# Second gate of a hybrid decoder layer: eight columns in the first feed-forward part instead of ten, their four sums at other output pairs, six columns beside the output projection

## The chip, the cores and the metric

One core of one Trainium2 chip runs the kernel. The metric is the device time of one execution in microseconds (us); the time of a kernel is the median of its runs. The profile shows one execution, instruction by instruction, with the engines TensorE (PE), VectorE (DVE), ScalarE (ACT), GpSimd (POOL) and SyncE (SP, which issues most of the DMAs).

## The reference, cut to what matters

```python
mod_all = jnp.einsum('bd,ldm->lbm', jax.nn.silu(c), w_ada) + b_ada[:, None, :]
sh1, sc1, g1, sh2, sc2, g2 = jnp.split(mod_all[l], 6, axis=-1)
h = modulate(rms_norm(x, norm1_g[l]), sh1, sc1)
u = h @ w_in[l]                      # convolution group and attention group
...
x = x + g1[:, None, :] * (mixed @ w_out[l])
h = modulate(rms_norm(x, norm2_g[l]), sh2, sc2)
x = x + g2[:, None, :] * (jnp.square(jax.nn.relu(h @ w_ff1[l])) @ w_ff2[l])
return rms_norm(x, normf_g)
```

There are 512 tokens of 2048 features in float32, and the feed-forward width is 8192. The second gate g2 has 2048 numbers. In the kernel they are 16 columns of 128 (one number per partition), kept in the last 16 columns of the tile `mod`. Each column is 128 dot products of a row of `w_ada` with SiLU(c), and the weights of one column are 1 MB. Nothing needs g2 before the end of the second feed-forward product, where it scales what is added to x.

## The kernel before, in words

The layer runs in three stages, each with an `Order` of its own: projections with convolution and values; attention; and then output projection with both feed-forward parts. Every operation is first recorded by `Order.record` (so that nearly all instructions have one line, L144, in the profile, and are told apart by their tiles), and `Order.emit` then calls a planner, `Order.plan`, that fixes the order of instructions on each engine. Tensor operations keep the order in which they were recorded. The others are taken when they are ready by the planner's own prices, and among those that are ready the one whose result is due first. For a DMA the planner counts its size at a fixed rate, a fixed latency, and `order.margin` on top: what reads the data is planned that much later. The third stage is planned in one pass. On the chip each engine then takes its instructions in the planned order and waits wherever something is not there yet.

Matmuls are done in three products of high and low halves (fp32r): ScalarE makes the high half of a weight block (`hl`), VectorE the low half. The feed-forward products use a Strassen-like scheme: seven block products for a 2 by 2 block product. The first feed-forward part makes 32 output pairs, p = 0 to 31: pairs 0 and 1 piece by piece ahead of the loop (`part`, `results_of`), pairs 2 to 31 in a loop over `ff1(p)`. One `ff1` loads four weight blocks of 512 KB through SP, adds two more to them in DMAs through POOL (up to p = 28; later pairs add on VectorE), runs 7 x 24 matmuls of 128x128 by 128x256, and stores its results to DRAM, through POOL.

The 16 columns of g2 are spread over the kernel:

- the first two (16 less `NLATE`) in the first stage;
- the columns from 16 less `NLATE` up to 16 less `NGATE` (the list `behind`) in `late_ada`, which is recorded first in the third stage and so runs beside the output projection. Each column takes two loads of 512 KB into four slots `wa`, and two VectorE dot products of 128x1024 (`dot`). The slots `wa`, and the two that hold SiLU(c), are used again later for the tokens of the feed-forward part (`tk`).
- the last `NGATE` in the loop over the pairs. `gate_part(s)` loads 256 KB of `w_gate` into the first half of the one tile `spare` (named `snap` in the trace) and adds its two halves, each times a column of SiLU(c), to one of the two running sums `gsums` in the second half of that tile. Eight parts make the sums of two columns, and `gate_sum(n)` lets TensorE add them over the partitions with a column of ones, after which VectorE adds the bias. The list `when` says behind which pair a part is recorded, and `sums` ahead of which pair a `gate_sum` is recorded, and so where it stands in TensorE's order.

`late_ada` and `gate_part` set `order.margin = MARGIN` around their loads.

With `NGATE` = 10 there are 40 parts and five sums, at p = 10, 15, 19, 24 and 28; `behind` has four columns.

Of the kernel before, what the change touches and what calls it, by code (L numbers as in the profile page):

```python
# [32 lines left out]
NWA = 8  # L33
NBANK = 6
NLATE = 14
NGATE = 10
NWARM = 3
SLACK = 4.0
MARGIN = 8.0
FAST = 378e3  # L40

V_BADA, V_N1, V_CW, V_CB, V_GC, V_GA, V_N2, V_NF, V_C, V_ID, V_END = \
# [272 lines left out]
def hybrid_layer(ctx: ExitStack, tc: tile.TileContext, a, out):  # L315
# [34 lines left out]
    def accum(name=None):  # L350
        return next(accums)
# [183 lines left out]
    for i in range(4):  # L535
# [8 lines left out]
        + [M_G2 * NK + k for k in range(NK - NLATE)]  # L544
    behind = [M_G2 * NK + k for k in range(NK - NLATE, NK - NGATE)]
    rb = accum("rb")
# [176 lines left out]
    def late_ada(n, slots):  # L723
# [4 lines left out]
        for k in range(n):  # L728
            m, acc = behind.pop(0), next(accs)
            for i in range(2):  # L730
                w = wa[(2 * k + i) % slots]
                order.margin = MARGIN
                nc.sync.dma_start(out=w, in_=a["w_ada"][2 * m + i])
# [123 lines left out]
    for j in range(8):  # L857
# [4 lines left out]
        for i in range(3):  # L862
            n = 3 * j + i
# [338 lines left out]
    def bankf():  # L1202
        return next(banks)
# [56 lines left out]
    for k in range(8):  # L1260
        wh, wl = oa[k] if k < 2 else hilo(hl_tile(16), raw_blob(a["w_oa"][k]))
        for i in range(8):
            s = slice(i * P, (i + 1) * P)
# [146 lines left out]
    def ff1(p):  # L1410
        raw = [raw_blob(a["w_f1"][p, b]) for b in range(4)]
        ps = {}
        x, y = temp((P, 2, HT), name="gx"), temp((P, 2, HT), name="gy")
        for i, w in enumerate(operands(raw, True, p % 4 == 3, add=[a["w_f1"][p, b] for b in (0, 3)] if p < 29 else None)):
            ch, first, last = CHAIN[i]
            if first:
                ps[ch] = bankf()
            run(ps[ch], w, tok[i], first, True)
            b = ps[ch][:, :HT]
            if i == B1:  # L1420
                p1 = next(p1s)
                nc.scalar.activation(p1, b, AF.Copy)
            elif i == U6:
                sub(y[:, 1], p1, b)
            elif i == T5:
                sub(y[:, 0], b, p1, OP.add)
            elif i == B2:
                nc.scalar.activation(x[:, 0], b, AF.Relu)
            elif i == T7:
                sub(y[:, 0], b, y[:, 0])  # L1430
            elif i == B3:
                sub(y[:, 1], b, y[:, 1], OP.add)
                nc.scalar.activation(y, y, AF.Relu)
                nc.scalar.activation(y, y, AF.Square)
            elif i == T4:
                sub(x[:, 1], b, p1)
                nc.scalar.activation(x[:, 1], x[:, 1], AF.Relu)
        nc.scalar.activation(x, x, AF.Square)
        outcome(p, x, y, [temp((P, 2, HT), name="gz") for _ in range(2)])
# [4 lines left out]
    NP = 2  # L1444
# [25 lines left out]
    def results_of(p):  # L1470
        x, y, z, v = [temp((P, 2, HT)) for _ in range(4)]
        for u in range(2):
            nc.scalar.activation(x[:, u], results[p, u][:, LO], AF.Relu)
            sub(y[:, 1 - u], firsts[p, u], results[p, u][:, HI], OP.add)
        nc.scalar.activation(x, x, AF.Square)
        nc.scalar.activation(y, y, AF.Relu)
        nc.scalar.activation(y, y, AF.Square)
        outcome(p, x, y, (z, v))

    def gate_part(s):  # L1480

        gsum, b = gsums[s // 8 % 2], s % 8
        order.margin = MARGIN
        nc.sync.dma_start(out=spare[:, :T], in_=a["w_gate"][s])
        order.margin = 0.0
        for j in range(2):
            w, c = spare[:, j * HT:(j + 1) * HT], sc[:, 2 * b + j:2 * b + j + 1]
            if b + j == 0:
                nc.vector.tensor_scalar(gsum, w, c, None, op0=OP.mult)
            else:  # L1490
                nc.vector.scalar_tensor_tensor(out=gsum, in0=w, scalar=c, in1=gsum, op0=OP.mult, op1=OP.add)

    def gate_sum(n):
        total, gsum = bankf(), gsums[n % 2]
        m = M_G2 * NK + NK - NGATE + 2 * n
        for i in range(2):
# [26 lines left out]
    for n in range(8, 16):  # L1523
        part(n)
        if n in (13, 15):
            results_of({13: 1, 15: 0}[n])
    when = [NP + 1 + s * 22 // (4 * NGATE) for s in range(4 * NGATE)]
    sums = [when[8 * n + 7] + 4 for n in range(NGATE // 2)]
    for p in range(NP, 32):
        if p in sums:  # L1530
            gate_sum(sums.index(p))
        ff1(p)
        for s in [s for s in range(4 * NGATE) if when[s] == p]:
            gate_part(s)
# [165 lines left out]
def _in_turn(np, m):  # L1700

    return np.arange(2 * m).reshape(2, m).T.reshape(-1)
# [21 lines left out]
def _layouts(np, x, c, w_ada, b_ada, norm1_g, w_in, conv_w, conv_b, cmp_pe_k, cmp_pe_v, cmp_w1_k,  # L1724
# [18 lines left out]
    d["xr"] = xt.reshape(NK // 2, P, 2, 2, T // 2)[..., _in_turn(np, W_F)].reshape(xt.shape)  # L1743
    early = D * 6 - P * NGATE
    d["w_ada"] = w_ada[0][:, :early].T.reshape(-1, P, 2, 1024).transpose(0, 2, 1, 3).reshape(-1, P, 1024)
# [51 lines left out]
```

## Time and profile before

| | us |
|---|---|
| median of 3 runs | 2088.17 |
| lowest and highest run | 2084.04, 2088.34 |
| the profiled execution | 2085.95 |
| its span, first to last instruction | 2084.2 |
| TensorE busy | 1989.4 (95%) |
| VectorE busy | 1807.3 (87%) |
| ScalarE busy | 1040.2 (50%) |

A line of an engine's view has the start in us, the duration, engine, line, operation, the tiles as out<-in with the kernel's names (tiles that share memory can appear under the other's name), shapes and the count; in brackets stands how long the engine was idle just before and what ended that. In a table of windows a row has, for each engine, its busy time in that stretch with the number of instructions in brackets, then the granted TensorE clock, the busy share of the 16 DMA engines and the GB/s that they moved.

### The profile page before, as it was taken

What the parts mean: (1) busy time and instruction counts of PE and PEld (TensorE: products, weight loads), DVE (VectorE), ACT (ScalarE), POOL (GpSimd) and SP (SyncE); (2) the same over time, 40 slices, a digit from 0 to 9 for tenths busy, and PEclk for the clock granted to TensorE, in tenths of its full rate; (3) what the DMA queues carried; (4) which work ended last, traced back from release to release, by engine and by line L of the source; (5) the groups of instructions that cost most, each with busy time, mean ns of one, the idle gap of its engine ahead of it and who ended that gap; (6) DMA issues with size and microseconds to landing.
All of it is one profiled execution on the core that took longest, in us unless ns stands there. A gap on an engine that the chain in (4) does not pass through costs nothing.

```text
span 2084.2 us, 37876 instructions
## 1 busy us (share of the span) xinstructions
PE 1989.4 (95%) x14950; PEld 1898.4 (91%) x14950; DVE 1807.3 (87%) x2684; ACT 1040.2 (50%) x1533; POOL 174.7 (8%) x288
## 2 busy tenths in 40 slices
PE   8999999999999999999979696969999999999997
PEld 6888888989888899999979696969999999999997
DVE  8999898888996689897968596869889999999997
ACT  5444433336774367665646364636644343434355
POOL 0000000000000011332222132211000000000000
PEclk9999999999999999999989798989999999999999
DMA  9896788885212836998978697857875576477582
GB/s 365 333 356 228 266 291 306 289 296 173 80 41 81 308 137 180 296 282 255 278 216 251 199 265 224 251 183 247 316 281 195 178 255 215 151 264 254 188 262 95
DMA packets 143522, 486.15 MB, mean 233 GB/s; under 512 B 17264, under 2 KB 21872, under 8 KB 143344
## 3 DMA queue, kind: packets, MB, share of 16 engines
q1 hardware_dynamic: 115952, 391.44, 52.0%
q0 software_dynamic: 26816, 91.24, 16.7%
q8 instruction: 117, 1.92, 0.4%
q10 hardware_dynamic: 576, 1.05, 0.1%
q14 instruction: 61, 0.50, 0.1%
HBM read 414.46 MB, written 69.21 MB: 232 GB/s over the span
## 4 chain that ended last, share of the span: by engine, by line
PE 85%; DVE 7%; DMA 3%; issue 3%; ACT 2%; POOL 0%; SPq 0%; DVEq 0%; ACTq 0%; POOLq 0%
PE pf L144 56%; PE ps L144 21%; PE pw L144 4%; PE s L144 1%; PE pv L144 1%; DMA snap<-in_w_gate 1%; DVE hl L144 1%; DVE t L144 1%; PE pt L144 1%; DVE xt L144 1%; DMA g<-gt 1%; DVE snap L144 1%; ACT hl L144 1%; DVE sg L144 0%; DVE sacc L144 0%
## 5 line engine op out<-in xcount | busy, mean ns | idle before, releaser
L144 PE MATMUL pf<-tk,hl 128*128 128x256 f32 x10656 | 1207.4, 277 | 3.2 <-ACT hl L144 1.2
L144 PEld LDWEIGHTS pf<-tk,hl 128*128 128x128 f32 x10656 | 1204.2, 194 | 4.8 <-issue 2.3
L144 ACT ACTIVATE hl<-rw 128x1024 fp32r<-128x1024 f32 x264 | 280.7, 1063 | 381.0 <-PE pf L144 335.7
L144 DVE TENSOR_TENSOR hl<-rw,hl 128x1024 fp32r<-128x1024 f32 x264 | 322.2, 1221 | 67.6 <-ACT hl L144 67.0
L144 ACT ACTIVATE hl<-sg 128x1024 fp32r<-128x1024 f32 x183 | 194.4, 1063 | 225.4 <-PE pf L144 211.7
L144 ACT ACTIVATE wh<-raw 128x1024 fp32r<-128x1024 f32 (+1 forms) x106 | 112.3, 1060 | 220.8 <-PE ps L144 170.9
L144 PE MATMUL ps<-h_m,wh 128*128 128x512 f32 x720 | 214.9, 379 | 0.0
L144 DVE TENSOR_TENSOR hl<-sg,hl 128x1024 fp32r<-128x1024 f32 x153 | 187.0, 1222 | 31.8 <-ACT hl L144 30.9
L144 PE MATMUL ps<-h,wh 128*128 128x512 f32 x560 | 165.8, 383 | 3.4 <-ACT h L144 2.6
L144 PEld LDWEIGHTS ps<-h_m,wh 128*128 128x128 f32 x720 | 135.0, 189 | 18.7 <-DVE h_m L144 0.2
L144 DVE TENSOR_TENSOR wl<-raw,wh 128x1024 fp32r<-128x1024 f32 (+1 forms) x106 | 130.0, 1226 | 16.5 <-ACT wh L144 15.3
L144 PE MATMUL ps<-h_m,wl 128*128 128x512 f32 x360 | 136.7, 380 | 0.0
L144 PEld LDWEIGHTS ps<-h,wh 128*128 128x128 f32 x560 | 106.1, 190 | 20.5 <-ACT h L144 4.2
L144 DVE CUSTOM_DVE_ANT_0 t<-wa,cs,vec 128x1024 bf16<-128x1024 f32 x86 | 110.3, 1283 | 13.4 <-DMA wa<-in_w_ada 12.6
L144 DVE CUSTOM_DVE_ANT_0 t<-wa,cs,acc 128x1024 bf16<-128x1024 f32 x86 | 110.3, 1283 | 6.4 <-DMA wa<-in_w_ada 5.9
L144 DVE TENSOR_TENSOR sg<-sg,rw 128x1024 f32<-128x1024 f32 x92 | 112.5, 1223 | 1.7
L144 POOL DMA_DIRECT2D g<-gt x180 | 97.6, 560 | 144.2 <-issue 64.9
L144 PE MATMUL ps<-h,wl 128*128 128x512 f32 x280 | 103.2, 381 | 0.0
L144 DVE TENSOR_TENSOR xt<-xt,pf 128x512 f32<-128x512 f32 x128 | 87.3, 683 | 12.6 <-PE pf L144 12.2
L144 PE MATMUL pw<-mix,wh 128*128 128x512 f32 x256 | 80.9, 387 | 0.0
L144 POOL DMA_DIRECT2D rw<-in_w_f x30 | 26.4, 881 | 644.2 <-ACT hl L144 535.3
L144 ACT ACTIVATE t<-t 128x512 f32<-128x512 f32 (+3 forms) x132 | 74.8, 567 | 6.5 <-DVE t L144 4.0
(244 smaller groups left out, 2298.7 us busy)
## 6 DMA issues: line engine op xcount, KB each, us to landing
rw<-in_w_f SPq DMA_DIRECT2D x260, 512.0 KB, 4.8
wa<-in_w_ada SPq DMA_DIRECT2D x172, 512.0 KB, 6.6
tk<-g SPq DMA_DIRECT2D x114, 512.0 KB, 6.5
g<-gt POOLq DMA_DIRECT2D x180, 256.0 KB, 6.5
raw<-in_w_conv SPq DMA_DIRECT2D x32, 512.0 KB, 4.6
rw<-in_w_f POOLq DMA_DIRECT2D x30, 512.0 KB, 6.5
sg<-in_w_f POOLq DMA_DIRECT2D x30, 512.0 KB, 5.5
snap<-in_w_gate SPq DMA_DIRECT2D x40, 256.0 KB, 5.8
```

Of the source, the lines that this page charges most:

```text
L144: x.i, x.eng, x.call = len(self.nodes), eng, (lambda: real(*args, **kw))
```

## The change

Three numbers and the two lists change. `NGATE` goes from 10 to 8: the loop has 32 parts and four sums, and `behind` has six columns, so that `late_ada` makes 12 loads and 12 dots where it made 8 of each. The parts are recorded behind pairs 3 to 24 as before, 16 of them for every 11 pairs where there were 40 for every 22, and the sums ahead of p = 12, 18, 25 and 30. `MARGIN` goes from 8.0 to 6.0 for the loads of both. The layout of the weights in DRAM follows `NGATE`.

```diff
-NGATE = 10
+NGATE = 8
 NWARM = 3
 SLACK = 4.0
-MARGIN = 8.0
+MARGIN = 6.0
 FAST = 378e3
...
-    when = [NP + 1 + s * 22 // (4 * NGATE) for s in range(4 * NGATE)]
-    sums = [when[8 * n + 7] + 4 for n in range(NGATE // 2)]
+    when = [NP + 1 + s * 11 // 16 for s in range(4 * NGATE)]
+    sums = (12, 18, 25, 30)
     for p in range(NP, 32):
         if p in sums:
             gate_sum(sums.index(p))
```

## The prediction

> **What bounds the kernel now.** I read the page first: engine shares, then the 40 slices.
>
> ```profile
> PE 1989.4 (95%) x14950; PEld 1898.4 (91%) x14950; DVE 1807.3 (87%) x2684; ACT 1040.2 (50%) x1533; POOL 174.7 (8%) x288
> ...
> PE   8999999999999999999979696969999999999997
> PEclk9999999999999999999989798989999999999999
> ```
>
> TensorE (PE) is the bound, and the slices show where it is not full: four notches, 7-6-6-6, between slices 21 and 27, which is the first feed-forward part, and the granted clock drops beside them. So I asked next for the tile of the gate work there. The trace calls it `snap`: loads of gate weights into it, two VectorE (DVE) steps per load, and four TensorE instructions per gate sum that read it.
>
> ```profile
> L144 DVE SCALAR_TENSOR_TENSOR snap<-snap,sc x75: 474/479/486, 845.0 to 1384.7; 128x256 f32<-128x256 f32 x75
> L144 SPq DMA_DIRECT2D snap<-in_w_gate x40: 327/328/924, 814.3 to 1381.7; - x40
> ...
>   PE pf L144: 71.1, 5
> ...
> DMA to landing us min/median/max: 2.4/5.8/8.8
> ```
>
> The third line is the finding: TensorE waited 71.1 us, in 5 waits, for VectorE's writes to this tile. There are five gate sums. The timeline of TensorE gives each wait in brackets:
>
> ```profile
> 965.92 1.01 PE L144 MATMUL pf<-ones,snap 128*128 128x1 f32 x4 [3.55 <-DVE snap L144]
> 1078.10 1.01 PE L144 MATMUL pf<-ones,snap 128*128 128x1 f32 x4 [15.10 <-DVE snap L144]
> 1176.12 1.02 PE L144 MATMUL pf<-ones,snap 128*128 128x1 f32 x4 [19.48 <-DVE snap L144]
> 1290.00 1.01 PE L144 MATMUL pf<-ones,snap 128*128 128x1 f32 x4 [16.11 <-DVE snap L144]
> 1385.23 1.01 PE L144 MATMUL pf<-ones,snap 128*128 128x1 f32 x4 [16.82 <-DVE snap L144]
> ```
>
> TensorE takes its queue in order, so a sum written ahead of pair 15 holds up every matmul of that pair until the eight loads behind it have been worked off. Why are they late? One part of the chain, from SyncE's (SP's) issues and VectorE's steps:
>
> ```profile
> 1002.26 0.47 SPq L144 DMA_DIRECT2D snap<-in_w_gate  x1
> 1017.43 0.33 SPq L144 DMA_DIRECT2D snap<-in_w_gate  x1
> ...
> 1015.29 0.47 DVE L144 SCALAR_TENSOR_TENSOR snap<-snap,sc 128x256 f32<-128x256 f32 x1
> 1016.92 0.48 DVE L144 SCALAR_TENSOR_TENSOR snap<-snap,sc 128x256 f32<-128x256 f32 x1
> ...
> L144 SPq DMA_DIRECT2D snap<-in_w_gate x6: 327/328/924, 865.2 to 952.0; - x6
> L144 SPq DMA_DIRECT2D snap<-in_w_gate x5: 328/328/468, 1002.3 to 1060.8; - x5
> ```
>
> The tile has one buffer, so loads go one by one: issued at 1002.26, first step at 1015.29 (13.0 us on, though a load lands in 5.8), second done at 1017.40, next issue at 1017.43. The 7 us between landing and step are the planner's MARGIN of 8.0, which places the steps that late in VectorE's order. From first to last issue the period is (952.0-865.2)/5 = 17.4 and (1060.8-1002.3)/4 = 14.6 us, so eight parts take some 130 us, while the old sums stand 4 or 5 pairs apart. The pair itself:
>
> ```profile
> 947.19 0.36 ACT L144 ACTIVATE p<-pf 128x256 f32<-128x256 f32 x1
> 972.77 0.36 ACT L144 ACTIVATE p<-pf 128x256 f32<-128x256 f32 x1
> ...
> 1010.29 0.36 ACT L144 ACTIVATE p<-pf 128x256 f32<-128x256 f32 x1
> 1029.05 0.36 ACT L144 ACTIVATE p<-pf 128x256 f32<-128x256 f32 x1
> ```
>
> This ScalarE copy comes once a pair: 18.76 us apart without a wait, 25.58 across the first sum. Five pairs are 94 us, four are 75; the chain cannot keep that up.
>
> **The change part by part.** *The waits.* Up to 71.1 us go if every sum is ready when TensorE gets there. It got to the first at 965.92-3.55 = 962.4, ahead of index 10. The new places are 12, 18, 25, 30, so without waits, at 18.76 a pair and 0.9 for each earlier sum, TensorE arrives at 999.9, 1113.3, 1245.5 and 1340.2. The chain starts at 814.3 as now. With MARGIN 6.0 every step is planned 2 us earlier, so I take 2 us off each period: the first eight took 965.9-814.3 = 151.6, now 135.6, ready at 950. For the others I take 16 as the old period (the middle of 14.6 and 17.4, as parts of both kinds occur), hence 14 and 112 us per sum: 1062, 1174, 1286. All four are ready 50 to 71 us early. With the old period they would come at 966, 1094, 1222 and 1350: only the last is late, by 10. So I take the full 71.1.
>
> *The slow clock behind each wait.* Windows of 20 us, one that starts with a sum and an ordinary one:
>
> ```profile
> core 0: us, PE busy (x) PEld busy (x) DVE busy (x) ACT busy (x) POOL busy (x), PEclk, DMA share, GB/s
> 1078.00:1098.00 20.00, 19.90 (x153) 19.91 (x154) 9.71 (x14) 6.19 (x8) 0.00 (x0) 0.85 0.33 104
> 1020.00:1040.00 20.00, 20.00 (x182) 20.00 (x181) 17.61 (x27) 13.14 (x18) 5.83 (x10) 1.00 0.99 304
> ```
>
> TensorE got 149 matmuls done besides the sum's four, instead of 182: 33 x 0.11 = 3.6 us, at a granted clock of 0.85. The ScalarE copies give 25.58-18.76-3.55 = 3.3 at the first. Five times 3.4 makes 17 us beyond the waits. The sums' own instructions remain: four sums at 0.5 to 0.9 us (1.01 is what one takes on the slow clock), some 3 us. Net 14 us. The Trainium skill (TensorE: Matmul & The Clock Gate, What's actually happening) says that the clock is halved after an idle window of about 3.4 us and returns after one busy window of the same length. By that each wait would lose 1.7 us afterwards, 8.5 in all, and the sum below would end some 6 us higher; the row shows the granted clock 0.15 short over 20 us, 3 us, and I go by the row.
>
> *Eight loads, sixteen steps, one sum fewer in the feed-forward part.* 16 x 0.48 = 7.7 us of VectorE and 2 MB go; nothing beyond the above, since VectorE is not what TensorE waits for there otherwise. The bank that a sum takes, and the add behind it, go once too: nothing. SP issues eight loads fewer, and none of its weight loads then stands behind them; POOL's queue is not touched.
>
> *Two columns more beside the output projection.* Four loads of 512 KB on SP and four VectorE dots.
>
> ```profile
> 690.00:716.00 26.00, 26.00 (x122) 22.75 (x121) 13.28 (x16) 7.40 (x7) 0.00 (x0) 1.00 0.95 359
> 716.00:741.00 25.00, 25.00 (x201) 24.28 (x200) 23.87 (x40) 12.55 (x19) 3.41 (x6) 1.00 0.68 245
> 741.00:749.00 8.00, 8.00 (x74) 7.97 (x73) 3.29 (x7) 2.40 (x5) 1.07 (x2) 1.00 0.18 69
> ...
> L144 SPq DMA_DIRECT2D wa<-in_w_ada x8: 327/328/652, 685.4 to 714.9; - x8
> L144 DVE CUSTOM_DVE_ANT_0 t<-wa,cs,acc x4: 1274/1279/1281, 703.2 to 729.0; 128x1024 bf16<-128x1024 f32 x4
> L144 DVE TENSOR_TENSOR tk<-x,tk x12: 682/684/695, 754.1 to 788.7; 128x512 fp32r<-128x512 f32 x12
> ```
>
> The dots cost 4 x 1.28 = 5.1 us, the loads 2.1 MB at 359 GB/s = 5.8 us. VectorE has 12.7 us free in the first window, 1.1 in the second and 4.7 in the third. The last dot starts at 729.0; a third round through the four slots, as long as one of the two now (half of 44), less what the margin saves, ends it near 745. The slots are then wanted for the tokens, first written at 754. TensorE has no idle time in these windows, so nothing can be gained. Ends: 0, and 5.1+5.8 = 11 if all of it lands on TensorE. I take 1, near the lower end, because of the 9 us to the tokens and the free time around. What hides it is that free time; if the order puts dots ahead of the updates that empty the PSUM banks (716 to 741), TensorE waits for those next.
>
> *The smaller MARGIN.* VectorE also takes its order in turn: a step that is planned before its load has landed stops all splits behind it, and then TensorE. The step shown stands 13.0 us behind the issue, with the margin 11; the longest landing is 8.8. So 0 (a landing of up to 11 costs nothing), upper end 32 parts x 0.5 us = 16 if landings get as long again as the spread from 5.8 to 8.8; I take 0.
>
> Sum against the profiled execution, 2085.95 us (span 2084.2 and 1.75 around it): 2085.95 - 71.1 - 14 + 1 = 2002. The three runs have their median at 2088.17, from 2084.04, so this execution lies 2 us below it.
>
> **The rivals.** *The chain gains nothing from the margin* (its steps wait for VectorE's next free place anyway): the last sum is late by 10 us plus 3.4 of slow clock, 2015; at a period of 17 us all through, by 34, 2040. For it: 17.4 in one stretch. Against: parts get shorter near a sum, as 14.6 shows.
>
> *Without the waits DMA becomes the bound.* The waits were also time in which transfers caught up.
>
> ```profile
> 814.00:1385.00 571.00, 499.10 (x4349) 497.39 (x4347) 457.64 (x671) 317.94 (x449) 151.21 (x246) 0.93 0.85 253
> 862.00:962.00 100.00, 100.00 (x897) 99.97 (x897) 89.69 (x130) 63.81 (x90) 28.12 (x46) 1.00 0.96 297
> ```
>
> 253 GB/s over 571 us and 26 pairs are 5.56 MB a pair; 0.1 MB less with the fewer gate loads, so 5.46 MB in 18.76 us, 291 GB/s. For 100 us the kernel held 297 at full TensorE, VectorE at 90%, which speaks against this rival; but the share of the DMA engines was 0.96 there. If capacity is 2 to 4% short over 28 pairs (525 us): 10 to 20 us, 2012 to 2022. The Trainium skill (DMA: Bandwidth & Descriptors, Where 436 GB/s comes from) has about 358 GB/s as a core's share of HBM, by which this rival could not be; the shares say that little is left at 297.
>
> *The waits only move with the sums*, because the planner puts off what is due later: four waits of 14.2 and 3.4 each remain instead of five, 2085.95 - 17.6 + 1 = 2069. Against it: the chain shown issues its next load 0.03 us after the second step, far ahead of the sum that needs it (1017 against 1078), and nothing is held back for the sum's sake.
>
> *Slower than before:* the smaller margin stops VectorE at every part. To eat the 84 us, each of 32 parts must stop TensorE for 2.6 us, so landings would have to reach 13.6 us on the average; the longest is 8.8.
>
> **How the numbers follow.** No wait left: 0.65, 2002 (1997 to 2010; 1996.9 is 2085.95-71.1-18, all gone and nothing paid). Margin without effect: 0.12. DMA: 0.13. Waits that move: 0.05. Slower: 0.03; 0.02 is for what I have not seen. Range 1996 to 2024, which leaves out the last three and the long end of the first rival. Faster 0.96, within 0.2% (4 us, about what these runs can tell) 0.01, slower 0.03.
>
> **What would show it.** Right: the tile of the gate has four sums, TensorE's waits for it under 3 us in all, no slice below 9 in the first feed-forward part, no clock drops there, and pairs 18.76 us apart from index 4 to 31. The last dot of the output projection ends before 750 with TensorE full there. The period of gate loads is near 14. Wrong: a bracketed wait at one of the four sums (rival one if at the last alone), pairs longer than 18.76 with waits for weights or stores (rival two), VectorE waiting for `snap` loads outside such gaps (the last).

## The result and the profile after

| | before | after |
|---|---|---|
| median, us | 2088.26 | 2026.58 |
| lowest and highest run | 2084.04, 2088.35 | 2022.53, 2027.81 |
| the profiled execution, its span | 2085.95, 2084.2 | 2027.81, 2025.4 |
| ratio to before, 95% interval | | 0.9706 [0.9688, 0.9724] |

The change made the kernel 3% faster. The forecast was 2002 with a range to 2024, so the direction and most of the size were right and the time lies 2.6 us outside. The page of the kernel after, at the lines shown of before:

```profile
PE 1982.6 (98%) x14946; PEld 1891.7 (93%) x14946; DVE 1807.4 (89%) x2675; ACT 1038.0 (51%) x1533; POOL 175.0 (9%) x288
...
PE   8999999999999999999999999979999999999998
PEclk9999999999999999999999999989999999999999
```

Four notches have become one, in slice 27. The tile of the gate and TensorE's timeline at the two sums that still waited (the other two show no bracket):

```profile
L144 SPq DMA_DIRECT2D snap<-in_w_gate x32: 327/328/486, 817.4 to 1348.5; - x32
...
  PE pf L144: 14.8, 3
...
DMA to landing us min/median/max: 2.8/5.1/7.9
```

```profile
1118.17 0.60 PE L144 MATMUL pf<-ones,snap 128*128 128x1 f32 x4 [0.98 <-DVE snap L144]
1357.81 1.02 PE L144 MATMUL pf<-ones,snap 128*128 128x1 f32 x4 [13.37 <-DVE snap L144]
```

The waits at the sums are down from 71.1 us to 14.4 (the third wait of the first view, under half a us, is at no sum). Nearly all of what is left stands at the last sum, where TensorE had to wait for the last gate part. The once-a-pair copies of ScalarE, the last three of after and then the last of before, show what that wait cost and what followed:

```profile
1329.26 0.36 ACT L144 ACTIVATE p<-pf 128x256 f32<-128x256 f32 x1
1364.95 0.37 ACT L144 ACTIVATE p<-pf 128x256 f32<-128x256 f32 x1
1384.15 0.37 ACT L144 ACTIVATE p<-pf 128x256 f32<-128x256 f32 x1
...
1448.62 0.37 ACT L144 ACTIVATE p<-pf 128x256 f32<-128x256 f32 x1
```

The pair with the last sum took 35.69 us, 16.9 more than a pair. From the last copy to the end the kernel took 2084.2-1448.62 = 635.6 us before and 2025.4-1384.15 = 641.2 now: the second feed-forward part, which the diff does not touch, has lost 5.6 us. And the copy of pair 5 comes at 877.41, before at 872.18: 5.2 us were lost by then. Against the forecast of 2002: 16.9 at the last sum less the 0.8 that I had allowed for it, 5.6 at the end and 4.2 at the start (5.2, of which 1 was forecast) make 2027.9, where the profiled execution took 2027.81. Two differences of 0.7 us, one in the loop and one outside the span, cancel in this.

So two questions: why the chain of gate parts was still late with 2 us less margin, and why the end lost 5.6 us.

### The profile page after: what moved, and what is told of

Its sections match the earlier page's. It is cut to its first block, busy times and chain, and to the rows that moved or that the text cites. A ratio compares the mean times of both kernels' runs of the same rounds, so it can differ in the third digit from the quotient of the medians.

```text
span 2025.4 us, 37894 instructions
## 1 busy us (share of the span) xinstructions
PE 1982.6 (98%) x14946; PEld 1891.7 (93%) x14946; DVE 1807.4 (89%) x2675; ACT 1038.0 (51%) x1533; POOL 175.0 (9%) x288
## 3 DMA queue, kind: packets, MB, share of 16 engines
q0 software_dynamic: 26816, 91.24, 17.1%
## 4 chain that ended last, share of the span: by engine, by line
PE 88%; DVE 7%; issue 2%; DMA 2%; ACT 1%; SPq 0%; DVEq 0%; POOL 0%; ACTq 0%
PE pf L144 60%; PE ps L144 20%; PE pw L144 4%; PE s L144 2%; PE pv L144 1%; DVE hl L144 1%; DVE xt L144 1%; DVE t L144 1%; PE pt L144 1%; DVE sg L144 1%; DMA raw<-in_cmp_w 1%; DVE sq L144 0%; DMA x<-in_xt 0%; DMA wa<-in_w_ada 0%; DVE wl L144 0%
```

## The experiments

A ratio compares a run with the kernel before as timed in the same round, where its median lay between 2085.4 and 2087.2 us.

**Does the margin set the pace of the parts?** Theory A: no, the place of the steps in VectorE's order does. The first run puts the margin back, the second changes the margin alone in the kernel before.

```diff
-MARGIN = 6.0
+MARGIN = 8.0
```

> The changed kernel with the margin back at 8.0; all else as changed. Theory A: in the stretches without urgency a gate part takes one pair time (18.7 us between first steps) because its steps get one free place per pair in VectorE's order; the margin does not set that period. Then the last sum is again late by about 13 us and the time is that of the changed kernel, 2027 us within 5. Rival B: the period is load plus margin plus steps, so 2 us more per part: 16 us over a group of eight, some 60 over all four, the third and fourth sums wait, the last by 30 to 45 us, 2045 to 2065 us.

```diff
 # in the kernel before
-MARGIN = 8.0
+MARGIN = 6.0
```

> The kernel before with the margin at 6.0 alone: 40 parts, five sums at their old places. Theory A: the waits at the sums stay as they were, 60 to 75 us in all, 2080 to 2092 us. Rival B: 2 us less per part, 16 per group of eight, takes most of each wait: 2010 to 2030 us.

Margin 8.0 in the changed kernel: 2041.22 us, 0.9785 of before [0.977, 0.9799]; the waits at the sums are 3.75, 6.15 and 14.27, 24.2 in all. Margin 6.0 in the old kernel: 2072.55, 0.9933 [0.9919, 0.9948]. Neither theory's number came out; both runs lie between. VectorE's timeline tells why. First the steps of three parts of the kernel after, then the first steps of the same three with margin 8.0:

```profile
907.19 1.00 DVE L144 SCALAR_TENSOR_TENSOR snap<-snap,sc 128x256 f32<-128x256 f32 x2
925.95 1.00 DVE L144 SCALAR_TENSOR_TENSOR snap<-snap,sc 128x256 f32<-128x256 f32 x2
944.71 1.00 DVE L144 SCALAR_TENSOR_TENSOR snap<-snap,sc 128x256 f32<-128x256 f32 x2
```

```profile
909.90 0.48 DVE L144 SCALAR_TENSOR_TENSOR snap<-snap,sc 128x256 f32<-128x256 f32 x1
...
928.67 0.47 DVE L144 SCALAR_TENSOR_TENSOR snap<-snap,sc 128x256 f32<-128x256 f32 x1
...
947.43 0.47 DVE L144 SCALAR_TENSOR_TENSOR snap<-snap,sc 128x256 f32<-128x256 f32 x1
```

Both have a period of 18.76 us, which is a pair: far from its sum a part gets one place per pair, and the margin changes nothing. The loads of this stretch in the kernel after:

```profile
L144 SPq DMA_DIRECT2D snap<-in_w_gate x6: 328/328/328, 871.9 to 964.5; - x6
...
DMA to landing us min/median/max: 4.2/4.6/5.5
```

They land 4.2 to 5.5 us after their issue, and the steps shown come 12 to 14 us later still. Close to a sum it is otherwise. The old kernel with margin 6.0 has these sums (the first no longer waits):

```profile
962.37 0.50 PE L144 MATMUL pf<-ones,snap 128*128 128x1 f32 x4
1073.02 1.01 PE L144 MATMUL pf<-ones,snap 128*128 128x1 f32 x4 [16.24 <-DVE snap L144]
1165.19 1.01 PE L144 MATMUL pf<-ones,snap 128*128 128x1 f32 x4 [14.50 <-DVE snap L144]
1276.16 1.02 PE L144 MATMUL pf<-ones,snap 128*128 128x1 f32 x4 [14.55 <-DVE snap L144]
1367.84 1.01 PE L144 MATMUL pf<-ones,snap 128*128 128x1 f32 x4 [13.21 <-DVE snap L144]
```

58.5 us of waits in place of 71.1. Its first parts nearly keep the old periods (18.2, 18.0, 16.2 and 16.4 us, where the kernel before has 18.3, 17.9, 16.3 and 16.4), and the two ahead of the first sum go in 13.4 and 12.4 where the old ones took 18.8 and 15.2. So the margin counts only for parts that have become urgent, that is, close to their due time, and theory A holds for the others alone.

**Are the places or the number of parts what helped?** Ten columns as before, with later sums:

```diff
 # in the kernel before
-    sums = [when[8 * n + 7] + 4 for n in range(NGATE // 2)]
+    sums = (11, 16, 20, 26, 31)
```

> The kernel before (ten columns, 40 parts, margin 8.0) with its five sums moved to pairs 11, 16, 20, 26 and 31. Theory A: the chain of 40 parts is as slow as before and the later places only take out part of the waits: about 46 us of waits remain instead of 71 (a part takes 16 us beside the pairs and 7.5 while TensorE waits, 814 + 40 x 16 against an arrival at 1356), 2055 to 2065 us. Rival D: the places were the cause and the number of parts does not matter: under 15 us of waits, 2025 or less.

2068.10 us, 0.9915 [0.9898, 0.9931], with waits of 14.55, 18.96, 7.65 and 15.12: 56.3 of the 71.1 stay, 10 more than forecast. Later places alone bring 19 us. One sum of the changed kernel moved one pair further:

```diff
-    sums = (12, 18, 25, 30)
+    sums = (12, 18, 25, 31)
```

> The changed kernel with the last sum ahead of pair 31 instead of 30. Theory A and B alike: the last eight parts end near 1358 us while TensorE would now arrive near 1363, so the wait of 13.4 us and the slow clock behind it (3.4) go: 2010 us. If instead the planner lets the parts slip with the sum that needs them (rival C: what is due later is done later), the parts end some 15 us later, a wait of 8 to 15 us remains and the time stays at 2020 to 2028.

2021.65 us, 0.9693 [0.9677, 0.971]. The last wait is still 10.0 us:

```profile
1372.09 1.01 PE L144 MATMUL pf<-ones,snap 128*128 128x1 f32 x4 [10.02 <-DVE snap L144]
```

It ends at 1372.1 instead of 1357.8. The sum stands one pair, 19 us, later, and its parts are done 14 us later: they slip with their deadline. That is rival C of the expectation, and the forecast of 2010 was wrong.

**Are the parts late because they are due late?** The planner takes, among what is ready, what is due first. Make the parts due at once:

```diff
     def gate_part(s):
         gsum, b = gsums[s // 8 % 2], s % 8
+        order.due = 0.1
         order.margin = MARGIN
 ...
+        order.due = None
```

> The changed kernel with the gate parts due at once in the planner (load and steps go ahead of everything else that is ready). Theory A: the parts lost time to VectorE's other work that was due earlier, so the period falls from 17 to about 12 us, all four sums are early, no wait is left: 2010 us or some us less, with at most 5 us given back where a step of 0.48 us delays a split. Rival B: the period is load plus margin plus steps and stays near 16; the last sum waits as before, 2027.

2007.37 us, 0.9624 [0.9609, 0.9638]. Loads from its gate tile, and its four sums:

```profile
L144 SPq DMA_DIRECT2D snap<-in_w_gate x32: 327/328/1311, 812.6 to 1220.4; - x32
```

```profile
998.49 0.51 PE L144 MATMUL pf<-ones,snap 128*128 128x1 f32 x4
1111.58 0.51 PE L144 MATMUL pf<-ones,snap 128*128 128x1 f32 x4
1246.38 0.51 PE L144 MATMUL pf<-ones,snap 128*128 128x1 f32 x4
1340.63 0.51 PE L144 MATMUL pf<-ones,snap 128*128 128x1 f32 x4
```

The period is (1220.4-812.6)/31 = 13.2 us, against (1348.5-817.4)/31 = 17.1 in the kernel after, with the same loads and the same margin. No sum waits, and they are reached at 998, 1112, 1246 and 1341, within 2 us of the prediction's arrivals. So the order set the pace of the chain, not the load. The order is not all of it at the start: the first seven periods are still 14.9 to 19.1 us although these parts are due first too, and only then do they fall to 9.6 to 14.5. What holds the early ones no run shows.

Why are they due late? The planner's backward pass counts a load with 2.9 us and its size, but not with the margin that its forward pass adds:

```diff
-            move = x.cost + x.lag if not x.size else 2.9 + x.size / Order.RATE
+            move = x.cost + x.lag if not x.size else 2.9 + x.margin + x.size / Order.RATE
```

> The changed kernel, with the margin counted in the due times too: the planner's backward pass, which says when a load is due, now takes 6 us more for each gate load, as its forward pass does already. Theory H: the last sum is late because eight parts are counted as about 37 us of lead while they take 110 to 130, so they become urgent too late; counted with the margin they are due some 85 us ahead, hurry earlier, and the last wait falls from 13 to under 4 us: 2008 to 2016 us. Rival: the parts are as fast as they can be once they are urgent, and the last wait stays near 13: 2022 to 2030.

2014.46 us, 0.9654 [0.9637, 0.9672], and at the last sum:

```profile
1346.46 0.61 PE L144 MATMUL pf<-ones,snap 128*128 128x1 f32 x4 [3.27 <-DVE snap L144]
```

13.4 us have become 3.3, as theory H said. The far parts of the first stretch still go at 18.7 to 18.8 us; the last eight become urgent earlier and take 10.2 to 13.9 each. So the due times decide, and their missing margin is 10 us of the last wait.

Is it the planner's holding rule (VectorE keeps a place empty when something due earlier is about to be ready) that keeps the parts out?

```diff
     nc = order = Order(tc, x1[0].tensor.tag, NMAIN)
-    order.waits = True
+    order.waits = False
```

> The changed kernel, planned in the third stage without the planner's rule by which VectorE and ScalarE leave a place empty when work that is due earlier becomes ready before the waiting step would be done. Theory A2: that rule is what leaves a gate part only one place per pair; without it the unhurried period falls from 18.8 to 15 us or less, the last sum is ready in time, and the time falls to 2008 to 2015 us unless splits are delayed by the steps. Rival C2: the place is set by the due times alone; the period stays at 18.8 in the unhurried stretches, the last wait stays near 13 us, 2022 to 2030.

2016.35 us, 0.9665 [0.965, 0.9679], between the two forecasts. The last wait is 11.37 us, 2 us less, and the fourth to the tenth period, far from the first sum, are still 18.1 to 19.0: theory A2 fails for the chain. Most of the gain came from elsewhere: the end took 634.9 us, not 641.2, and the copy of pair 5 came 3.2 us earlier.

**What happened to the end?** Three runs go with it. First the loop without any gate parts:

```diff
-        order.margin = MARGIN
-        nc.sync.dma_start(out=spare[:, :T], in_=a["w_gate"][s])
-        order.margin = 0.0
-        for j in range(2):
+        if b == 0:
+            nc.vector.memset(gsum, 0.0)
+        for j in range(0):
```

> The changed kernel without the gate parts: no gate loads and no steps in the first feed-forward part, the running sums are zeroed once and summed as before, so that eight columns of the second gate hold their bias alone. It is the floor for this loop. All theories: no wait at a sum, pairs of 18.76 us, 2004 to 2009 us. If the parts also cost the loop VectorE or DMA time beside the waits at the sums, it comes out 5 us or more below the 2007 of the kernel with the parts first. If the 5 to 6 us that the second feed-forward part lost came from the gate parts, they are gone here and it ends near 1999; if they come from the order planned behind a loop without waits, they stay.

2007.05 us, 0.9619 [0.9605, 0.9633]: the same as with the parts first. From the copy of pair 4 to the last copy this kernel takes 508.2 us and the one with the parts first 511.0, but the next two runs, which have the parts, take 508.0 and 507.9. So the parts need not cost the loop anything beside their waits, neither through VectorE nor through DMA. And the end takes 640.7 us without them, so they are not what slows it. Then the parts first, with all due times of the stage 70 us earlier:

```diff
+    order.early = 70.0        # third stage, with the parts first
...
-        t, ideal, fixed, best = 0.0, {}, None, None
+        t, ideal, fixed, best = -self.early, {}, None, None
```

> The kernel with the parts first, and all due times of the third stage 70 us earlier in the plan, as far as the old kernel's plan lagged by its waits at the sums. Theory F: the 5.6 us that the second feed-forward part lost (635.6 to 641.2 from the last pair to the end) come from the planner's holding rule, which compares due times with the plan's clock and changes when the plan no longer lags; then they return to 636 and the time is near 2002 us. Rival G: the order of the last blocks comes out differently with any change in the plan; then the time is 2003 to 2012 and that stretch has no relation to the lag.

2002.09 us, 0.9596 [0.9579, 0.9613], and 635.2 us for the end. And the parts first without the holding rule:

```diff
-    order.waits = True
+    order.waits = False       # third stage, with the parts first
```

> The kernel with the parts first, planned in the third stage without the holding rule. Theory F: the second feed-forward part takes 635 us from the last pair to the end instead of 641, with no waits at the sums: 2000 to 2003 us. If the holding rule is needed once VectorE is tighter with the parts first, waits for splits take 3 us or more in the loop and it ends at 2004 to 2010.

1998.88 us, 0.958 [0.9565, 0.9594], the fastest of all, with 634.7 us for the end. What TensorE waited for from the last pair on (us in total, times, longest), in the kernel after, and with the due times 70 us earlier:

```profile
PE pf L144 <- DVE xt L144: 5.6, 3, 2.8
PE pf L144 <- DVE rs L144: 0.6, 1, 0.6
```

```profile
PE pf L144 <- ACT hl L144: 1.2, 1, 1.2
PE pf L144 <- DVE xt L144: 0.6, 2, 0.4
```

All thirteen kernels side by side (the waits are those in brackets at the sums, the end is the span less the time of the last copy, as above):

| kernel | waits at the sums, us | the end, us |
|---|---|---|
| before | 71.1 | 635.6 |
| before, margin 6.0 | 58.5 | 636.1 |
| before, later places | 56.3 | 635.2 |
| after, margin 8.0 | 24.2 | 636.4 |
| after | 14.4 | 641.2 |
| after, last sum at 31 | 11.0 | 639.6 |
| after, margin in the due times | 3.3 | 642.1 |
| parts first | 0 | 641.1 |
| ten columns, parts first | 0 | 640.3 |
| no parts | 0 | 640.7 |
| parts first, due times 70 us earlier | 0 | 635.2 |
| after, no holding rule | 11.4 | 634.9 |
| parts first, no holding rule | 0 | 634.7 |

Kernels with over 20 us of waits, or without the holding rule, or with due times that lie as far behind the plan's clock as the old waits put them, have 634.7 to 636.4 us; the rest have 639.6 to 642.1. From the last pair on, TensorE waits for `xt` 0.6 to 1.0 us in the seven of the first kind (2.9 in the one with 24.2 us of waits) and 5.1 to 6.8 in the six others. By its code the rule compares due times with the clock of the plan, and keeps a place empty only if the work that it keeps it for will be done by the due time of the step that it passes over. When the plan lags, nearly everything is overdue and the rule hardly acts; without the lag it acts, and TensorE waits for VectorE's updates of `xt` in the second feed-forward part. The two runs that switch the effect off, by earlier due times and without the rule, give back the 6 us and the short waits for `xt`, which bears theory F out. That the plan lagged by as much as the chip waited is argued: no view shows the plan's own clock.

**Were fewer columns needed?** Ten columns, four beside the output projection, margin 6.0, the parts first:

```diff
 # in the kernel before; gate_part as in the run with the parts first
-MARGIN = 8.0
+MARGIN = 6.0
-    sums = [when[8 * n + 7] + 4 for n in range(NGATE // 2)]
+    sums = (11, 16, 20, 26, 31)
```

> Ten columns in the loop again (40 parts, four columns beside the output projection), margin 6.0, the parts due at once, sums at pairs 11, 16, 20, 26 and 31. If the order of the parts is what decides and their number does not, 40 parts at 13 us end near 1335, ahead of the last sum at 1356, and no wait is left: 2003 to 2010 us. If fewer parts were needed, the chain falls behind and waits of 10 us or more stand at some sums: 2020 us or more.

2008.25 us, 0.9625 [0.961, 0.9639], no wait at any sum, the 40 parts done at 1315. Against 2007.37 with eight columns (0.9624) there is no difference, so fewer columns were not needed once the order was right. With the slow chain they seem to help: at margin 8.0 the ratio is 0.9785 with eight columns and 0.9915 with ten and later places, though the sums of these two do not stand at the same pairs.

## Why the prediction was right and wrong, by its steps

*The waits were the price, and most of them went:* right. 56.7 of 71.1 us are gone. Nothing new took their place on VectorE or DMA in the loop. The rival of DMA as the bound falls with the run without parts, and with the pairs of the kernel after, which take 18.76 us nearly everywhere that no sum stands.

*"With MARGIN 6.0 every step is planned 2 us earlier, so I take 2 us off each period":* this step failed. I had read the 7 us between landing and step as the margin. They were the wait for a place in an order by due times, which in the kernel after comes once a pair in the stretch shown: 18.76 us with either margin. The four groups of eight parts were to be done at 950, 1062, 1174 and 1286; they were done at 977, 1118, 1249 and 1358. The first and the third were still ahead of TensorE, by 27 and 1 us; the second was 1 us late and the fourth 13.4.

It is nearest to the first rival (the margin gains nothing because the steps wait for a place), which had 0.12 and was priced at 2015 to 2040. That the time lies in its price is in part luck: its wait at the last sum gives 2018, and the rest came from the end and the start. The old stretch of 17.4 us was the row to go by, not the middle between it and 14.6, because later sums leave more parts far from theirs. The rival that the waits move with the sums had 0.05 for all four. The run with the last sum at 31 shows that it is true in part, 14 us of 19. What was held against it, the next load 0.03 us after the second step, showed only that loads are not held back; the steps were.

*The slow clock, 3.4 us behind each wait:* right. The window that starts at the last sum:

```profile
1358.00:1378.00 20.00, 20.00 (x151) 20.00 (x152) 9.03 (x12) 5.96 (x8) 1.22 (x3) 0.83 0.39 132
```

35.69-18.76-13.37 = 3.56 us beyond the wait, the 1.0 us of the sum's own instructions included. In windows of 2 us the granted clock is 0.50 from 1361 to 1363 and 1.00 from 1365 to 1367; 0.83 over 20 us makes (1-0.83) x 20 / 0.5 = 6.8 us at half speed, and a loss of 3.4. The 1.7 us that I had worked out from the Trainium skill (TensorE: Matmul & The Clock Gate, What's actually happening) are half of that, here as before. The sum that I said would end some 6 us higher by that rule ends 8.5 higher if 8.5 takes the place of 17 and nothing else changes.

*Two columns more beside the output projection, 1 us:* the place was right.

```profile
716.00:741.00 25.00, 25.00 (x194) 24.06 (x193) 24.09 (x38) 10.35 (x14) 2.87 (x5) 1.00 0.87 331
741.00:749.00 8.00, 8.00 (x73) 7.85 (x71) 6.76 (x15) 4.16 (x8) 1.62 (x3) 1.00 0.32 132
...
L144 DVE CUSTOM_DVE_ANT_0 t<-wa,cs,acc x6: 1277/1278/1279, 705.0 to 738.7; 128x1024 bf16<-128x1024 f32 x6
```

The last dot ends at 740, TensorE is full, and VectorE took the dots in the time it had free (6.76 busy of 8.00 where it was 3.29). Yet the copy of pair 5 was 5.2 us later than before, where I had put 1. The columns are not shown to be the cause: with the same six, the parts-first kernel has that copy at 870.9, 1.3 us earlier than before, and with four columns and the parts first it comes at 876.6. It differs from order to order, and why is open.

*The end:* this is the second step that failed, a term put at nothing without a reason. I took what the diff does not touch as unchanged, but the order there hangs on the holding rule and on how far the plan lags, and a change that removes waits takes the lag away too. It cost 5.6 us. The late chain alone would have left the time near 2018, within the range; with the end it is 2024, and with the start 2028.

## What to carry to other kernels

When a chain of small steps is late under a list scheduler, ask first when the scheduler thinks that they are due: a period that equals the loop's own suggests that they are served once a round. Here a smaller margin then gained nothing far from a sum and a later deadline only in part, while an earlier due time brought a part from 17.1 to 13.2 us. Count every allowance that the forward pass makes in the backward pass too. And when a change removes a stall from a planned program, look at the stages behind it as well: their order can depend on the stall.

## What the runs showed of the hardware

From 3.55 us of waiting on, the loss behind a wait (the sum's own instructions included) hardly grows with the wait: 3.27 us at the first sum of before (waited 3.55), 3.56 at the last of after (waited 13.37), and 2.6 to 3.6 at all 19 such waits of these runs, up to 19.48 us long. Shorter waits lost less: 1.96 us behind 3.27 us in the run with the margin in the due times (granted clock 0.91 over the next 20 us), 0.71 behind 0.98 us in the kernel after (1.00). The four instructions of a sum took 0.50 or 0.51 us where TensorE came without a wait, 0.60 or 0.61 behind a wait of 0.96 to 3.27 us, and 1.01 or 1.02 from 3.55 us on. And the DMA engines did not become the bound when the waits went: the loop of the fastest kernel ran at 279 GB/s up to the last pair, with a busy share of the DMA engines of 0.91 and TensorE busy for 548.14 of 550 us.

```profile
814.00:1364.00 550.00, 548.14 (x4907) 547.82 (x4906) 499.57 (x729) 357.04 (x506) 159.91 (x262) 1.00 0.91 279
```
